# Strassen input sums on one engine, and sums, gate reductions and pairs moved, in a fused decoder-layer kernel

## The chip, the cores and the metric

The kernel runs on one core of a Trainium2 chip. Its inputs and output are in the chip's memory, everything is fp32, and the matrix engine is fed the fp32r type: each operand is split into a high part and a low remainder, and three matmuls (high by high, high by low, low by high) make one product. The metric is the device time of one execution in microseconds (us); lower is better. Three executions of the kernel before took 934.26, 934.66 and 939.55 us.

The engines are called by their profile names: PE is TensorE (matmuls; PEld its weight loads), DVE VectorE, ACT ScalarE, POOL GpSimd, and SP SyncE, whose queue issues nearly all DMAs in order.

## The reference

One decoder layer on 1024 tokens of width 1024, cut to what is computed:

```python
mod = c @ w_ada + b_ada; shift, scale, gate = split(mod, 3)
h = rms_norm(x, g_pre) * (1 + scale) + shift
proj = h @ w_in                 # 5144 columns: queries, keys, values, SiLU gates, merge gates
q_a, kv_c, kv_s, kv_w, g_nsa, z_a, q_b, kv_b, z_b, merge = split(proj, pts)
# mixer A: compressed (an MLP over blocks), selected and window-512 attention, 8 heads, 2 kv heads
o_a = gts[0] * o_cmp + gts[1] * o_slc + gts[2] * o_win
y_a = (merge_heads(o_a) * silu(z_a)) @ w_o_nsa
# mixer B: window-128 attention with sinks, 8 heads, 2 kv heads
o_b = banded_attention(q_b, k_b, v_b, slopes_b, 128, sinks=sinks)
y_b = (merge_heads(o_b) * silu(z_b)) @ w_o_swa
m_a, m_b = split(merge, 2)
y = (sigmoid(m_a) * y_a + sigmoid(m_b) * y_b) @ w_out
out = x + gate * rms_norm(y, g_post)
```

## The kernel before, in words

Features lie on the 128 partitions and tokens along the free dimension, in two halves of 512 tokens. `hh` and `hl` are the high and low parts of the normalised input h, eight blocks of 128 features by two halves. The weight matrix w_in is cut into named blocks of 128 columns: Q and K blocks, `ZA0..3` and `ZB0..3` (SiLU gates), and `MA0..7`, `MB0..7` (merge gates).

The order of the work: normalise x and project values, the first keys and queries (to about 90 us); the Z blocks and the compression MLP (`mlp`, L630, two sides), side by side to about 181 us; then four units of attention, `("B", 0), ("B", 1), ("A", 0), ("A", 1)`, to about 722 us; then the last matrix products with the merge gates and w_out. A scheduler orders the instructions of each engine from priorities (program order, raised or lowered by `high_priority`) and a simulated clock; on the chip each engine and each DMA queue then runs its list in that fixed order, and waits at the first instruction that isn't ready.

**Attention.** A unit runs eight query blocks. `scores` (L790) makes the scores on PE, bias and row minimum on DVE (L862), the exponential on ACT (L874), the row scales (for mixer B with two 128x4 tensor_tensor instructions on DVE, L880 and L882) and the scaling on POOL (L886). `weigh` (L910) transposes on PE (L923), splits on ACT and DVE (L929, L930) and multiplies by V on PE (L931, L934). `finish` (L936) loads the SiLU gate `zt`, adds the two halves of the result into `ot` (ACT L943, DVE L944), multiplies on POOL (L945) and stores; `zt` and `ot` have one buffer each. Between these steps projection products of later Q, K and merge-gate blocks are put in: in the B units whole blocks (`proj_half`, L193, matmuls at L200 to L208, weights split by ACT L174 and POOL L177), in the A units halves of products (`Part`, L969), spaced by a plan in units of PE columns.

**The merge gates by Strassen.** Two of the 16 merge-gate blocks (`PLAIN`, MB0 and MB1) are projected plainly; the other 14 are taken as seven pairs (`PAIRS`). A pair (a, b) is a 2x2 block product with h split into two feature halves and two token halves, done in seven products in place of eight. It needs sums of the four weight quarters (S1 to S4, `pair_sums`, L697: four 128x512 tensor_tensor on POOL, each stored) and sums of the four quarters of h (T1 to T4).

- `early_sums` (L712) makes the weight sums of pairs 0 to 2 ahead of attention, in four of the eight `q` buffers (the first queries hold the other four); `late_sums` (L1139) makes those of pairs 3 to 6 in the B units, two a unit, in `ps` buffers that the scores use too.
- `input_sums(k)` (L719, k = 0 to 3) follows them in the same four `q` buffers: two loads of h, two adds on POOL (L726), four sums on DVE (L727 to L730), then for each T a high part on ACT (L733), the low part on DVE or POOL in turn (L735), and two stores (L736, L737).
- `new_set` (L1035) loads a T, high and low, over parts of `hh` and `hl` that are no longer used, in the last two units. `middle_products` and `last_products` use them; the last products (T3 and T4) of pairs 3 to 6 come behind attention, in the "seam" (L1289 to L1306), where the finished second block of each pair is stored, to be loaded again as a gate.

**The gated products.** Behind the seam eight reductions (L1308 to L1326) make the post-norm gate from w_ada: eight loads of 512 KB and 11 reductions on DVE (L1322). Then `gated` (L1328) runs for m = 0 to 7 on side B and again on side A: it loads a w_o block, makes two products of 12 matmuls (L1336 to L1338), and multiplies each by a merge gate that `merge_gate` (L1273) loads and puts through a sigmoid. Between them the w_out rows are loaded and formed into the sums of another Strassen product.

Of the kernel before, what the change touches and what calls it, by code (L numbers as in the profile page):

```python
# [14 lines left out]
P = 128  # L15
# [50 lines left out]
EARLY = 3  # L66
# [4 lines left out]
def hybrid_kernel(tc, io, out):  # L71
# [84 lines left out]
    t_dram = {n: [[dram.tile([P, HS], F32, name=f"{n}{x}{k}", tag=f"{n}{x}{k}") for x in "hl"] for k in range(KH)]  # L156
# [555 lines left out]
    def early_sums(p):  # L712

        quads = [t.bitcast(F32) for t in spare(4)]
        for t, (name, j) in zip(quads, ((PAIRS[p][0], 0), (PAIRS[p][0], 1), (PAIRS[p][1], 0), (PAIRS[p][1], 1))):
            nc.sync.dma_start(t.rearrange("p (k t) -> p k t", k=KH), quarter_of(name, j))
        pair_sums(p, *quads)
# [218 lines left out]
    def finish(mixer, g, i, pv):  # L936
        zt = at.tile([64, 4, P], F32, name="zt", tag="zt", bufs=1)
# [201 lines left out]
    def late_sums(p):  # L1139

        a, b = (at.tile([P, S], F32, name="ps", tag="ps", bufs=4) for _ in range(2))
        for t, name in zip((a, b), PAIRS[p]):
            nc.sync.dma_start(t.rearrange("p (k t) -> p k t", k=KC), io["w_blk"][W_IDX[name]])
        pair_sums(p, a[:, :HS], a[:, HS:], b[:, :HS], b[:, HS:])
# [547 lines left out]
```

## Time and profile before

| | before |
|---|---|
| time, three executions | 934.26, 934.66, 939.55 us |
| profiled execution: its time, its span | 934.04 us, 931.5 us |
| PE busy | 879.4 us (94%), 4418 matmuls |
| DVE, ACT, POOL busy | 676.9, 530.2, 504.4 us |
| mean granted TensorE clock | 0.974 of full speed |
| DMA | 164.06 MB, mean 176 GB/s |

The span runs from the first instruction to the last; the 2.54 us between span and time lie around it. The profile takes one execution; that one is 0.62 us below the median. "Busy" of PE counts a matmul from its start to a modelled end, and neighbours overlap, so that how fast matmuls follow one another tells more than the busy share. [...]

### The profile page before, as it was taken

The numbers are of one execution on the slowest core, as the hardware profiler recorded it, in microseconds if no ns is written. First come the engines' busy times: TensorE is split into PE (matmuls) and PEld (weight loads), VectorE is DVE, ScalarE is ACT, GpSimd is POOL, SyncE is SP. The second block draws the span as 40 slices with busy tenths as digits, with TensorE's granted clock in tenths as the row PEclk, the third lists the DMA queues.
The fourth block names the chain that finished last, engine by engine and source line by source line (L and its number), as shares of the span: only waits on it lengthen the run. The fifth ranks groups of instructions, "written<-read, shape, count | busy, mean of one in ns | idle before, by whom it ended". The sixth has DMA issues, their size and how long they took to land.

```text
span 931.5 us, 14888 instructions
## 1 busy us (share of the span) xinstructions
PE 879.4 (94%) x4418; PEld 736.0 (79%) x4418; DVE 676.9 (73%) x1651; ACT 530.2 (57%) x1200; POOL 504.4 (54%) x523
## 2 busy tenths in 40 slices
PE   9999989849998989999999999999999969989994
PEld 7889778637887878788888888888887858877884
DVE  5866965884688867766677677777674578788996
ACT  6487423444676687766567686666564237453241
POOL 1001862594876887645346486654553229854541
PEclk9999999959999999999999999999999989999998
DMA  9966684855545543121132754423462899951322
GB/s 352 316 234 216 211 282 170 290 210 151 194 149 168 158 151 108 58 91 69 46 103 67 276 174 127 134 91 114 162 212 91 286 403 342 324 175 35 102 91 113
DMA packets 99058, 164.06 MB, mean 176 GB/s; under 512 B 11553, under 2 KB 29345, under 8 KB 98978
## 3 DMA queue, kind: packets, MB, share of 16 engines
q1 hardware_dynamic: 97824, 161.89, 51.3%
q10 hardware_dynamic: 1154, 1.23, 0.5%
q8 instruction: 35, 0.57, 0.2%
q14 instruction: 45, 0.37, 0.1%
HBM read 115.10 MB, written 44.30 MB: 171 GB/s over the span
## 4 chain that ended last, share of the span: by engine, by line
PE 74%; DVE 12%; DMA 6%; issue 3%; ACT 2%; POOL 2%; SPq 1%; DVEq 0%; POOLq 0%; ACTq 0%
PE b_pt L923 7%; PE b_pj L990 6%; PE b_pj L996 6%; PE b_pj L995 6%; PE b_pv L934 4%; PE b_s L855 4%; PE b_s L852 4%; PE b_pv L931 4%; PE b_pj L200 3%; PE b_pj L207 3%; PE b_pj L208 3%; DMA wa<-in_w_adaT 2%; PE b_s L223 1%; PE b_s L225 1%; PE b_s L224 1%
## 5 line engine op out<-in xcount | busy, mean ns | idle before, releaser
L177 POOL TENSOR_TENSOR wl<-wraw,wh 128x512 fp32r<-128x512 f32 x123 | 167.9, 1370 | 102.3 <-ACT wh L174 72.7
L930 DVE TENSOR_TENSOR pl<-b_pt,ph 128x512 fp32r<-128x512 f32 x162 | 110.4, 686 | 42.0 <-ACT ph L929 41.3
L929 ACT CAST ph<-b_pt 128x512 fp32r<-128x512 f32 x162 | 93.6, 583 | 60.4 <-PE b_pt L923 51.9
L174 ACT CAST wh<-wraw 128x512 fp32r<-128x512 f32 x115 | 70.2, 618 | 52.9 <-PE b_pj L995 24.2
L874 ACT ACTIVATE ps<-ps,mins 128x256 f32<-128x256 f32 (+7 forms) x128 | 81.0, 634 | 32.5 <-DVE mins L862 29.1
L852 PE MATMUL b_s<-kh,q 128*128 128x256 f32 (+6 forms) x272 | 86.8, 327 | 12.0 <-DVE mins L862 11.3
L200 PE MATMUL b_pj<-hh,wh 128*128 128x512 f32 x208 | 84.0, 404 | 9.3 <-ACT wh L174 6.0
L886 POOL TENSOR_SCALAR ps<-ps,rr,gates 128x128 f32<-128x128 f32 (+7 forms) x64 | 52.5, 824 | 65.5 <-DVE rr L878 53.3
L855 PE MATMUL b_s<-kl,q 128*128 128x256 f32 (+6 forms) x272 | 83.5, 316 | 0.0
L208 PE MATMUL b_pj<-hh,wl 128*128 128x512 f32 x208 | 82.7, 399 | 0.6 <-POOL wl L177 0.6
L207 PE MATMUL b_pj<-hl,wh 128*128 128x512 f32 x208 | 82.8, 398 | 0.0
L990 PE MATMUL b_pj<-hh,wh 128*128 128x512 f32 x188 | 77.7, 413 | 0.0
L996 PE MATMUL b_pj<-hh,wl 128*128 128x512 f32 x188 | 74.2, 395 | 0.0
L995 PE MATMUL b_pj<-hl,wh 128*128 128x512 f32 x188 | 74.2, 395 | 0.0
L923 PE MATMUL b_pt<-ident,ps 128*128 128x128 f32 x408 | 69.7, 281 | 1.1 <-POOL ps L886 0.9
L934 PE MATMUL b_pv<-pl,V 128*128 128x512 f32 x162 | 69.3, 428 | 0.4 <-DVE pl L930 0.2
L931 PE MATMUL b_pv<-ph,V 128*128 128x512 f32 x162 | 67.0, 414 | 1.7 <-DVE ot L944 1.5
L852 PEld LDWEIGHTS b_s<-kh,q 128*128 128x128 f32 x272 | 51.7, 190 | 21.2 <-DVE mins L862 13.1
L923 PEld LDWEIGHTS b_pt<-ident,ps 128*128 128x128 f32 x408 | 52.8, 144 | 12.2 <-POOL ps L886 1.7
L886 POOL TENSOR_SCALAR pw<-pw,rr,gates 128x640 f32<-128x640 f32 (+4 forms) x64 | 47.5, 744 | 24.5 <-DVE rr L878 20.1
L855 PEld LDWEIGHTS b_s<-kl,q 128*128 128x128 f32 x272 | 51.8, 191 | 6.6
L200 PEld LDWEIGHTS b_pj<-hh,wh 128*128 128x128 f32 x208 | 40.0, 192 | 18.5 <-ACT wh L174 7.6
(446 smaller groups left out, 2468.7 us busy)
## 6 DMA issues: line engine op xcount, KB each, us to landing
wraw<-in_w_blk SPq DMA_DIRECT2D x83, 256.0 KB, 3.1
wa<-in_w_adaT SPq DMA_DIRECT2D x20, 512.0 KB, 5.2
r<-in_w_out SPq DMA_DIRECT2D x32, 256.0 KB, 5.1
wraw<-sS SPq DMA_DIRECT2D x28, 256.0 KB, 2.9
w1raw<-in_w SPq DMA_DIRECT2D x16, 256.0 KB, 4.0
ps<-in_w_blk SPq DMA_DIRECT2D x8, 512.0 KB, 4.8
sS<-ps SPq DMA_DIRECT2D x16, 256.0 KB, 2.3
od<-ot SPq DMA_DIRECT2D x64, 64.0 KB, 2.1
```

The source lines that it names most:

```text
L177: chain("wl", nc.gpsimd.tensor_tensor(wl, raw, wh.bitcast(F32), ALU.subtract))
L200: ins = nc.tensor.matmul(t, lhsT=wh, rhs=hh[kc][half], start=(kc == 0), stop=False)
L207: nc.tensor.matmul(t, lhsT=wh, rhs=hl[kc][half], start=False, stop=False)
L208: nc.tensor.matmul(t, lhsT=wl, rhs=hh[kc][half], start=False, stop=(kc == KC - 1))
L852: ins = nc.tensor.matmul(sp[:, :n_in], lhsT=q, rhs=rh, start=True, stop=False)
L855: nc.tensor.matmul(sp[:, :n_in], lhsT=q, rhs=rl, start=False, stop=True)
L923: ins = nc.tensor.transpose(t[:, r * P : r * P + P], rows[r][:, off : off + P], ident)
L930: nc.vector.tensor_tensor(pl, t, ph.bitcast(F32), ALU.subtract)
L934: nc.tensor.matmul(pv, lhsT=v, rhs=pl, start=False, stop=(last and n == len(todo) - 1))
L990: ins = nc.tensor.matmul(self.t, lhsT=wh[:, kc, :], rhs=hi, start=(self.first is None and kc == 0), stop=False)
L995: nc.tensor.matmul(self.t, lhsT=wh[:, kc, :], rhs=lo, start=False, stop=False)
L996: ins = nc.tensor.matmul(self.t, lhsT=wl[:, kc, :], rhs=hi, start=False, stop=(kc == KH - 1 and self.stop))
```

## The change

- **Order of the pairs.** `PLAIN` becomes MA6, MA7, and the pairs are (MA0, MA1), (MA2, MA3), (MA4, MA5), then (MB4, MB0) to (MB7, MB3). The seam now finishes MB0 to MB3; it puts them through the sigmoid there and keeps them in SBUF (`early`), where `gated` takes them; they are no longer stored and loaded. T3 and T4 products of a pair follow one another.
- **Weight sums.** None ahead of attention. `late_sums` takes pairs 0 and 1 in the first unit (steps 0 and 4) and pair 2 in the second, at lowered priority. `paced_sums` takes pairs 3 to 6 in the third unit, in `kts` and `kt` buffers, loads and sums at planned points.
- **Input sums.** All six sums of `input_sums` are on POOL, and each T is stored once, not split. `set_load` loads a T into the place of its low part, and `set_form` splits it (ACT copy, POOL subtract) in the last unit, ahead of given parts of the plan.
- **Gate reductions.** The eight w_ada blocks are reduced ahead of attention, behind the input sums, in 16 halves of 128x512 through the three `wraw` buffers, which the weights of the projections use too; c is broadcast into two `kt` buffers.
- **Heads.** `finish` of mixer B takes `zt` and `ot` from the four `pw` buffers, so two of each.

```diff
-PLAIN = ["MB0", "MB1"]
-PAIRS = [("MB2", "MB3"), ("MB4", "MB5"), ("MB6", "MB7")] + [(f"MA{m}", f"MA{m + 4}") for m in range(4)]
+PLAIN = ["MA6", "MA7"]
+PAIRS = [("MA0", "MA1"), ("MA2", "MA3"), ("MA4", "MA5")] + [(f"MB{m + 4}", f"MB{m}") for m in range(4)]
...
+    gate_c, gate_part = [], sm.tile([P, 8], F32, name="gpart")
+    for h in range(2):
+        gate_c.append(kq.tile([P, HS], F32, name="cg", tag="kt", bufs=6))
+        nc.sync.dma_start(gate_c[h], io["c"][h * HS : h * HS + HS].partition_broadcast(P))
+    def gate_sum(k):
+        blk, part = 16 + k, gate_part[:, k : k + 1]
+        for h in range(2):
+            wa = wp.tile([P, HS], F32, name="wraw", tag="wraw", bufs=3)
+            nc.sync.dma_start(wa, io["w_adaT"][blk * P : blk * P + P, h * HS : h * HS + HS])
+            nc.vector.tensor_tensor_reduce(
+                out=wa, in0=wa, in1=gate_c[h], scale=1.0, scalar=part if h else smalls[:, 8 + blk : 9 + blk],
+                op0=ALU.mult, op1=ALU.add, accum_out=mod[:, blk : blk + 1] if h else part)
     def input_sums(k):
...
-            nc.gpsimd.tensor_tensor(t, hh[kk][0].bitcast(F32), hl[kk][0].bitcast(F32), ALU.add)
-        nc.vector.tensor_tensor(b22, b22, b12, ALU.subtract)
-        nc.vector.tensor_tensor(b12, b12, b11, ALU.subtract)
-        nc.vector.tensor_tensor(b11, b22, b11, ALU.add)
-        nc.vector.tensor_tensor(b21, b21, b11, ALU.subtract)
-        for n, (name, t) in enumerate((("T3", tiles[3]), ("T1", tiles[2]), ("T2", tiles[0]), ("T4", tiles[1]))):
-            hi = wp.tile([P, HS], F32R, name="wh", tag="wh", bufs=WBUFS)
-            nc.scalar.copy(hi, t.bitcast(F32))
-            eng = nc.gpsimd if n % 2 else nc.vector
-            eng.tensor_tensor(t, t.bitcast(F32), hi.bitcast(F32), ALU.subtract)
-            nc.sync.dma_start(t_dram[name][k][0], hi.bitcast(F32))
-            nc.sync.dma_start(t_dram[name][k][1], t.bitcast(F32))
-    for p in range(EARLY):
-        early_sums(p)
+            op_(t, hh[kk][0].bitcast(F32), hl[kk][0].bitcast(F32), ALU.add)
+        op_(b22, b22, b12, ALU.subtract)
+        op_(b12, b12, b11, ALU.subtract)
+        op_(b11, b22, b11, ALU.add)
+        op_(b21, b21, b11, ALU.subtract)
+        for name, t in (("T3", b22), ("T1", b12), ("T2", b11), ("T4", b21)):
+            nc.sync.dma_start(t_dram[name][k], t)
     for k in range(KH):
         input_sums(k)
+    for k in range(8):
+        gate_sum(k)
+    nc.vector.tensor_tensor(amod, mod[:, 16:24], g_post, ALU.mult)
...
+        if mixer == "B":
+            zt, ot = (at.tile([64, 512], F32, name=n, tag="pw", bufs=4) for n in ("zb", "ob"))
...
+    def set_form(name, ks):
+        for k in ks:
+            hi, lo = sets[name][k]
+            nc.scalar.copy(hi, lo.bitcast(F32))
+            nc.gpsimd.tensor_tensor(lo, lo.bitcast(F32), hi.bitcast(F32), ALU.subtract)
...
+    def paced_sums(p):
+        quads = {}
+        def get():
+            a11, a12 = (kq.tile([P, HS], F32, name="sa", tag="kts", bufs=8) for _ in range(2))
+            a21, a22 = (kq.tile([P, HS], F32, name="sb", tag="kt", bufs=6) for _ in range(2))
+            quads[0] = a11, a12, a21, a22
+            for n, t in ((2, a21), (3, a22), (0, a11), (1, a12)):
+                nc.sync.dma_start(t.rearrange("p (k t) -> p k t", k=KH), quarter_of(PAIRS[p][n // 2], n % 2))
+        return get, lambda: pair_sums(p, *quads[0])
...
-            for n in range(2):
-                p = EARLY + 2 * u + n
-                if p < NP:
-                    at_step.setdefault(1 + 4 * n, []).append(lambda p=p: late_sums(p))
+            for p in ((0, 1), (2,))[u]:
+                at_step.setdefault(4 * (p % 2), []).append(lambda p=p: late_sums(p))
...
+                for n, p in enumerate(range(FIRST, NP)):
+                    for f, share in zip(paced_sums(p), (0.02, 0.07)):
+                        pieces.append((begun + whole[u] * (share + 0.14 * n), lambda at, f=f: f()))
...
+                for n, (name, ks) in enumerate((("T2", (0, 1)), ("T2", (2, 3)), ("T1", (0, 1)), ("T1", (2, 3)))):
+                    ahead_of(line[2 + n], lambda name=name, ks=ks: set_form(name, ks))
...
+                for k in range(KH):
+                    ahead_of(line[11 + k], lambda k=k: set_form("T3", (k,)))
...
+                ahead_of(e[1][0], lambda: set_form("T4", range(KH)))
...
-            store(half_of(PAIRS[p][1], 1), e)
-            seam.append((p, y))
-        for p, y in seam:
-            t = seam_part(load_half(quarter_of(PAIRS[p][1], 1)), sets["T4"])
+            nc.scalar.activation(e, e, AF.Sigmoid)
+            t = seam_part(load_half(quarter_of(b, 1)), sets["T4"])
             nc.vector.tensor_tensor(y, y, t, ALU.add)
-            store(half_of(PAIRS[p][1], 0), y)
-        cbg = op.tile([P, D], F32, name="cbg", tag="oh3")
...
-                nc.sync.dma_start(wa, io["w_adaT"][blk * P : blk * P + P, n * w : n * w + w])
...
+            nc.scalar.activation(y, y, AF.Sigmoid)
+            early[b, 1], early[b, 0] = e, y
...
+                if (name, half) in early:
+                    sg = early[name, half]
```

## Rows read from the trace of the kernel before

**Rows 1.** The page's head and the busy time of the engines (us, share of the span, instructions).

```profile
span 931.5 us, 14888 instructions
...
PE 879.4 (94%) x4418; PEld 736.0 (79%) x4418; DVE 676.9 (73%) x1651; ACT 530.2 (57%) x1200; POOL 504.4 (54%) x523
```

**Rows 2.** Busy time by stretch. The columns are: the stretch, its length, then busy us (x instructions) of PE, PEld, DVE, ACT and POOL, the granted TensorE clock (1.00 is full speed), the busy share of the 16 DMA engines, and GB/s.

```profile
116.00:140.00 24.00, 20.98 (x89) 16.83 (x88) 14.36 (x17) 6.62 (x10) 14.98 (x12) 0.93 0.85 282
140.00:163.00 23.00, 23.00 (x128) 20.00 (x127) 13.63 (x22) 6.96 (x13) 6.04 (x5) 1.00 0.47 168
...
176.00:210.00 34.00, 17.94 (x70) 13.01 (x69) 30.84 (x58) 17.76 (x49) 29.68 (x32) 0.65 0.70 253
...
280.00:303.00 23.00, 20.53 (x103) 16.92 (x102) 19.18 (x44) 15.01 (x41) 16.00 (x21) 0.93 0.51 163
...
530.00:625.00 95.00, 94.96 (x524) 80.95 (x523) 72.09 (x274) 68.16 (x188) 63.67 (x82) 1.00 0.41 130
...
755.00:770.00 15.00, 7.39 (x26) 5.66 (x25) 12.49 (x24) 7.88 (x14) 6.37 (x4) 0.77 1.05 398
770.00:820.00 50.00, 50.00 (x222) 41.39 (x222) 40.10 (x45) 29.38 (x52) 44.40 (x29) 1.00 0.95 326
```

**Rows 3.** What PE waited for over the whole span: the waiting line, what released it, us in total, times, longest us.

```profile
PE b_s L852 <- DVE mins L862: 11.3, 5, 5.1
PE b_pj L1336 <- ACT wh L174: 7.6, 1, 7.6
PE b_pj L200 <- ACT wh L174: 6.0, 1, 6.0
...
PE b_pv L931 <- DVE ot L944: 1.5, 1, 1.5
```

**Rows 4.** From the timelines of DVE, ACT and POOL near 200 us: start, us from there to the end of the last of the merged instructions, engine, line, what it writes and reads, how many.

```profile
197.23 4.84 DVE L729 TENSOR_TENSOR q<-q 128x512 f32<-128x512 f32 x1
...
203.43 1.66 ACT L174 CAST wh<-wraw 128x512 fp32r<-128x512 f32 x3
...
197.22 1.26 POOL L945 TENSOR_TENSOR ot<-ot,zt 64x512 f32<-64x512 f32 x1
198.46 1.83 POOL L886 TENSOR_SCALAR ps<-ps,rr 128x256 f32<-128x256 f32 x4
200.26 1.26 POOL L735 TENSOR_TENSOR q<-q,wh 128x512 fp32r<-128x512 f32 x1
```

**Rows 5.** The instructions of the input sums, grouped by line, from 80 to 210 us, where all of them lie: count, busy us in total, mean ns of one, idle time of the engine before them and what ended it.

```profile
L735 POOL TENSOR_TENSOR q<-q,wh 128x512 fp32r<-128x512 f32 x8 | 11.1, 1387 | 21.1 <-ACT wh L733 21.1
L726 POOL TENSOR_TENSOR q<-hh,hl 128x512 f32<-128x512 f32 x8 | 10.7, 1338 | 8.2 <-DMA T2l<-q 7.0 <-DMA sS<-q 0.8 <-DMA T4l<-q 0.3
L733 ACT CAST wh<-q 128x512 fp32r<-128x512 f32 x16 | 9.7, 619 | 17.4 <-DVE q L727 6.1 <-issue 3.9 <-DMA T3h<-wh 2.1
...
L735 DVE TENSOR_TENSOR q<-q,wh 128x512 fp32r<-128x512 f32 x8 | 7.9, 1003 | 2.5 <-ACT wh L733 2.5
L729 DVE TENSOR_TENSOR q<-q 128x512 f32<-128x512 f32 x4 | 7.6, 1890 | 0.0
...
L727 DVE TENSOR_TENSOR q<-q 128x512 f32<-128x512 f32 x4 | 4.0, 1011 | 4.3 <-DMA q<-h1d 4.3
L728 DVE TENSOR_TENSOR q<-q 128x512 f32<-128x512 f32 x4 | 3.3, 814 | 0.1
L730 DVE TENSOR_TENSOR q<-q 128x512 f32<-128x512 f32 x4 | 2.7, 681 | 0.0
```

**Rows 6.** From the timelines of DVE and POOL in the second half of the B units; of POOL the first and the last of four instructions in a row (the others are L704 and L177).

```profile
280.76 4.92 DVE L882 TENSOR_TENSOR sums<-sums,rr 128x4 f32<-128x4 f32 x1
...
280.63 1.29 POOL L945 TENSOR_TENSOR ot<-ot,zt 64x512 f32<-64x512 f32 x1
...
284.38 1.27 POOL L706 TENSOR_TENSOR ps<-ps 128x512 f32<-128x512 f32 x1
```

**Rows 7.** Where the stage ahead of attention begins and ends for POOL (its first weight sum, and attention's first scaling), the two last loads into `wraw` ahead of attention on SP's queue, and three kinds of DMA: KB each and median us from issue to landing.

```profile
93.38 3.31 POOL L700 TENSOR_TENSOR q<-q 128x512 f32<-128x512 f32 x1
...
179.72 1.95 POOL L886 TENSOR_SCALAR ps<-ps,rr 128x128 f32<-128x128 f32 x3 [0.41 <-DVE rr L883]
...
139.91 0.33 SPq L164 DMA_DIRECT2D wraw<-in_w_blk  x1
...
143.02 0.33 SPq L164 DMA_DIRECT2D wraw<-in_w_blk  x1
...
wraw<-in_w_blk SPq DMA_DIRECT2D x83, 256.0 KB, 3.1
...
q<-h1d SPq DMA_DIRECT2D x8, 256.0 KB, 3.5
...
T4l<-q SPq DMA_DIRECT2D x4, 256.0 KB, 3.3
```

**Rows 8.** The gate reductions: of the instructions of L1322 the 128x512 ones (ns least/median/most), and SP's queue from 741 us on.

```profile
L1322 DVE CUSTOM_DVE_ANT_0 r<-r,cbg,smalls x3: 746/746/746, 755.8 to 758.7; 128x512 f32<-128x512 f32 x3
...
741.89 3.25 SPq L1320 DMA_DIRECT2D wa<-in_w_adaT  x3
...
750.78 2.90 SPq L1320 DMA_DIRECT2D r<-in_w_adaT  x4
...
756.54 0.33 SPq L164 DMA_DIRECT2D wraw<-in_w_o  x1
```

More of the change, by code (lines that the diff above doesn't have):

```diff
@@ L62 @@
 W_NAMES, W_COLS = w_blocks()
-PLAIN = ["MB0", "MB1"]
-PAIRS = [("MB2", "MB3"), ("MB4", "MB5"), ("MB6", "MB7")] + [(f"MA{m}", f"MA{m + 4}") for m in range(4)]
+PLAIN = ["MA6", "MA7"]
+PAIRS = [("MA0", "MA1"), ("MA2", "MA3"), ("MA4", "MA5")] + [(f"MB{m + 4}", f"MB{m}") for m in range(4)]
 NP = len(PAIRS)
-EARLY = 3
+FIRST = 3
 LOOK = 3
@@ L155, in hybrid_kernel @@
     h_dram = [dram.tile([P, HS], F32, name=f"h1d{k}", tag=f"h1d{k}") for k in range(KC)]
-    t_dram = {n: [[dram.tile([P, HS], F32, name=f"{n}{x}{k}", tag=f"{n}{x}{k}") for x in "hl"] for k in range(KH)]
+    t_dram = {n: [dram.tile([P, HS], F32, name=f"{n}d{k}", tag=f"{n}d{k}") for k in range(KH)]
               for n in ("T1", "T2", "T3", "T4")}
@@ L710, in spare @@
         return [kq.tile([P, HS], F32R, name="q", tag="q", bufs=8) for _ in range(n)]
[L712 to L717, printed above, removed]
+    gate_c, gate_part = [], sm.tile([P, 8], F32, name="gpart")
[10 more added lines that the diff above has]
+                op0=ALU.mult, op1=ALU.add, accum_out=mod[:, blk : blk + 1] if h else part)
     def input_sums(k):
-        tiles = spare(4)
-        b11, b21, b12, b22 = (t.bitcast(F32) for t in tiles)
+        op_ = nc.gpsimd.tensor_tensor
+        b11, b21, b12, b22 = (t.bitcast(F32) for t in spare(4))
         nc.sync.dma_start(b12, h_dram[k])
@@ L936, in finish @@
     def finish(mixer, g, i, pv):
-        zt = at.tile([64, 4, P], F32, name="zt", tag="zt", bufs=1)
+        if mixer == "B":
+            zt, ot = (at.tile([64, 512], F32, name=n, tag="pw", bufs=4) for n in ("zb", "ob"))
+            zt = zt.rearrange("d (r t) -> d r t", r=4)
+        else:
+            zt = at.tile([64, 4, P], F32, name="zt", tag="zt", bufs=1)
+            ot = at.tile([64, 512], F32, name="ot", tag="ot", bufs=1)
         for p in range(2):
@@ L1033, in hybrid_kernel, with set_load @@
     sets = {}
-    def new_set(name, j, half):
-        res = []
+    def set_load(name, j, half):
+        sets[name] = res = []
         for k in range(KH):
@@ L1040, in new_set, with ahead_of, both @@
             pair = [main.tile([P, HS], F32R, name=f"{x}t{kk}", tag=f"{x}{kk}_{half}") for x in ("hh", "hl")]
-            for t, src in zip(pair, t_dram[name][k]):
-                nc.sync.dma_start(t.bitcast(F32), src)
+            nc.sync.dma_start(pair[1].bitcast(F32), t_dram[name][k])
             res.append(pair)
-        sets[name] = res
+    def set_form(name, ks):
[3 more added lines that the diff above has]
+            nc.gpsimd.tensor_tensor(lo, lo.bitcast(F32), hi.bitcast(F32), ALU.subtract)
+    def ahead_of(part, f):
+        was = part.before
+        def both():
+            f()
+            if was:
+                was()
+        part.before = both
     def t_set(name):
@@ L1139, in late_sums @@
     def late_sums(p):
[L1141 to L1144, printed above, removed]
+        with tc.high_priority(offset=-PRIO):
+            a, b = (at.tile([P, S], F32, name="ps", tag="ps", bufs=4) for _ in range(2))
+            for t, name in zip((a, b), PAIRS[p]):
+                nc.sync.dma_start(t.rearrange("p (k t) -> p k t", k=KC), io["w_blk"][W_IDX[name]])
+            pair_sums(p, a[:, :HS], a[:, HS:], b[:, :HS], b[:, HS:])
+    def paced_sums(p):
[7 more added lines that the diff above has]
+        return get, lambda: pair_sums(p, *quads[0])
     late = []
@@ L1209, in hybrid_kernel @@
                                    lambda at, f=f, k=k, ahead=ahead: f.piece(k, at, ahead)))
+            pieces.sort(key=lambda x: x[0])
         prev = None
@@ L1287, in seam_part @@
             return t
-        seam = []
+        early = {}
         for n, p in enumerate(range(NP - 4, NP)):
+            b = PAIRS[p][1]
             if n < 2:
@@ L1338, in gated @@
                     nc.tensor.matmul(ty, lhsT=wo[1][:, k, :], rhs=o_h, start=False, stop=(k == 3))
-                sg = tmp("t2", 4)
-                merge_gate(name, half, sg)
+                if (name, half) in early:
+                    sg = early[name, half]
+                else:
+                    sg = tmp("t2", 4)
+                    merge_gate(name, half, sg)
                 emit(sl, ty, sg)
```

26 lines of the change are left out of this document (4 added, 22 removed).

## The prediction

> **What bounds the kernel now.** I read the page's totals, then busy time by stretch, then what PE waits for, and last the timelines at the places these point to. PE is the bound, and its busy share hides how far from it single stretches are, so I count matmuls. From 140 to 163 us, full clock, PE issues 128 in 23.0 us, 0.18 us each for a mix of shapes; from 770 to 820 us 222 of 512 columns in 50.0 us, 0.225 us each [rows 2]. Against these two paces four stretches stand out:
>
> - 176 to 210 us, the start of attention: 70 matmuls in 34.0 us at a granted clock of 0.65. At 0.18 they need 12.6: **21.4 us lost**.
> - 755 to 770 us, the gated products: 26 in 15.0 us at 0.77. At 0.225 they need 5.9: **9.1 us lost**.
> - 280 to 303 us, in the B units: 2.5 us without a matmul and a clock of 0.93, another 1.6: **4.1 us lost**.
> - 116 to 140 us, Z blocks and MLP: 3.0 us without one and 0.93, another 1.7: **4.7 us lost** [rows 2].
>
> In the A units PE stands still for 0.04 us of 95; nothing is to be had there [rows 2]. In the first stretch PE waits for the row minima on DVE and for ACT's copies of the K weights (11.3 and 6.0 us over the span [rows 3]). Why these are late is in the timelines: DVE's L729, an input sum, takes 4.84 us where L730 takes 0.68, and ends just after a run of POOL instructions, 197.2 to 201.5 us; ACT copies the K weights only at 203.4, behind copies for the input sums that waited for that DVE instruction [rows 4, 5]. So the input sums, standing in DVE's and ACT's lists among attention's first steps, cost most of the 21.4 us. In the second stretch PE waits 7.6 us for a w_o block [rows 3]: its load is issued at 756.5, behind the loads for the gate reductions on SP, with the DMA engines full (share 1.05) [rows 2, 8].
>
> **The change, part by part.** The sum runs against the profiled execution: span 931.5 us [rows 1], and 2.54 around it.
>
> *Input sums.* DVE loses 24 instructions, 7.9 + 7.6 + 4.0 + 3.3 + 2.7 = 25.5 us, ACT 16 copies, 9.7 us, and POOL 8 subtractions, 11.1 us, all ahead of or inside the gap; POOL gains 16 sums at the price of its present adds, 1.34 us, 21.4 us [rows 5]. Stores fall from 32 to 16, and the 12 weight sums of POOL, with 24 DMAs, leave the stage. With one set of four buffers the sums stay a chain: a load 3.5, six sums 8.0, the last store 3.3 us, so 14.8 for each k and 59 for four. From 93.4, where POOL now starts its weight sums, that ends at 153; attention first needs POOL at 179.7 [rows 5, 7]. The 27 us between are room for the Z weights' splits. What then stands in the gap are attention's own steps and a pair of weight sums, as in the other B stretches. The nearest row is 280 to 303 us: 4.1 lost in 23, so 6.1 in 34 us [rows 2]. I take a gain of **15**; the ends are 0 (something else fills the gap) and 21.4.
>
> On this trace the DVE ops that go take 1.06 us each on average, since POOL holds them up, and 0.68 at their fastest, against POOL's 1.34 [rows 5]. [...]
>
> *Gate reductions moved.* 16 x 0.75 = 12 us of DVE [rows 8] come ahead of attention, where 25.5 us leave. Their 16 loads go through three `wraw` buffers ahead of the K weights, whose last two loads ahead of attention now stand at 139.9 and 143.0. A turn is 3.1 + 0.75 us, so 16 / 3 turns take 20.5 us, to 160.4, and K's loads land by 164, well before attention's first scaling at 179.7 [rows 7, 8]; until then PE has Z products. Price **0** under that cover; without it, the second rival.
>
> *Seam and gated products.* Eight loads of 512 KB and c go, eight stores and eight loads of 256 KB too: 8.5 MB, or 21 us at the 398 GB/s of that stretch [rows 2]. The w_o load no longer stands behind them. I take a gain of **8** of 9.1; the 1.1 is for the sigmoid, which now comes earlier on ACT. Ends: 0 and 9.1.
>
> *B units.* Two head buffers take away PE's wait for `ot`, 1.5 us [rows 3]; the second unit has one pair's weight sums instead of two. A lock-out like L882's, 4.92 us behind four POOL instructions [rows 6], becomes rarer, and it is what the 4.1 us are made of. I take a gain of **2**. Ends: 5.6 (both), and a loss of 1.5, since sums at lowered priority may keep two of the four `ps` buffers longer.
>
> *Ahead of attention.* Twelve more sums of POOL, 16 us net, run beside the MLP. From 116 to 140 us PE lost 4.7 us with POOL 15.0 us busy [rows 2]; in proportion that is 5 more. DVE has less to do there, which could give the 4.7 back. I take a loss of **2**, nearer to the upper end, as every POOL sum can hold a DVE one. Ends: a gain of 4.7, a loss of 5.
>
> *A units.* The third gets 16 weight sums, 21.4 us of POOL, the fourth 16 splits, 22.2 us of POOL and 9.7 of ACT [rows 5]. POOL is 67% busy there and PE never waits [rows 2], so most is hidden. The exposed piece is T4's: four splits in a row, 5.5 us, one part of the plan ahead of their use. I take a loss of **2**; ends 0 and 10.9 (that, and four weight sums in a row ahead of a scaling).
>
> Sum: 931.5 - 15 - 8 - 2 + 2 + 2 = 910.5, and 2.5 around it: **913 us**. The profiled execution's time, 934.04, is 0.6 below the median of 934.66, so this is 2.3% below the median. With every term at its lower end it would be 893.
>
> **The rivals.**
>
> *The gap stays, for POOL* (0.10). The 24 sums take longer than 59 us, by the Z splits and by DVE, and still run when attention starts; POOL's list then holds up the scalings. For it: 32 us of work on an engine already 30 of 34 us busy there [rows 2]. Against it: 27 us of room. With the whole gap 928 us, with half of it 920.
>
> *The gap stays, for the weights' buffers* (0.10). If the 16 gate loads come one by one, held by SP's order or by DVE, they take 16 x 3.85 = 62 us, from 139.9 to 201.5, and the K weights are copied about where they are now, at 203.4 [rows 4, 7]. A wait would take the place of the one removed: 928, or 920 with half. Against it: three buffers, and DVE with 9.4 us of idle time from 140 to 163 [rows 2].
>
> *No gain at the seam* (0.08). Heads and w_out rows also load there, and the DMA share is still 0.95 from 770 to 820 us [rows 2]; if the products wait for these, 921.
>
> *Slower: DVE locked out by POOL ahead of attention* (0.06). A gate reduction reads two operands from SBUF, as L729 and L882 do, and these were held 4.2 and up to 4.9 us by runs of POOL instructions [rows 4, 6]. POOL now has runs of six sums. At one sum each 16 reductions wait 16 x 1.34 = 21 us, at 4.8 each 77; halfway 49, of which 9.4 fit into DVE's idle time. The minima of the first scores stand behind them on DVE. That is 913 + 40 = 953, and it decides from 21 us that reach PE.
>
> [...]
>
> **How the numbers follow.** Forecast 0.62, with a range of its own of 903 to 921; better than 899, with the gap nearly closed, 0.04; the rivals 0.34 as given. The range from **899 to 929** leaves out the slower rival, the very good end and some of the bounds at either end. What this kernel's measurement can tell from no change is about 1%, 9.3 us. Below 925.3 lie the forecast, the better end, the seam rival and some six of the twenty parts of the two gap rivals: **0.80**. Within 1% the rest of these: **0.14**. Above: **0.06**.
>
> **What would show it.** Right: from 176 us on no DVE tensor_tensor of the input sums, K's copies on ACT before 180, a clock of 1.00 in place of 0.65; after 735 us no wait of L1336 of several us, and DMA below 0.9. First rival: POOL still in the input sums behind 176. Second: PE's L200 waiting for L174, and `wraw` loads of w_ada on SP behind 176. Third: L1336 waits for DVE's or ACT's heads. Slower: gate reductions far above 0.75 us with the scores' minima behind them. A loss in the A units would show as waits of PE for L177 or L886 where there are none. The prediction is wrong if the gap from 176 closes and the time doesn't follow.

## The result, and the profile after

The changed kernel takes **905.97 us** (median of four runs, 902.27 to 906.57); the kernel before, run beside it on the same chip, 935.82 (934.26 to 939.55). The ratio is **0.967**, with a 95% interval of 0.963 to 0.971. The profiled execution took 906.57 us, with a span of 904.7. Against 913 forecast the gain is 7 us larger, and inside the range. First the head of the page after and its engines [rows 1]:

```profile
span 904.7 us, 14788 instructions
...
PE 872.4 (96%) x4418; PEld 731.0 (81%) x4418; DVE 659.8 (73%) x1637; ACT 530.0 (59%) x1200; POOL 537.4 (59%) x547
```

PE's work is the same 4418 matmuls, DVE has 17 us less and POOL 33 more. Where it tells is in the stretches, the same seven as in [rows 2], columns as there:

```profile
116.00:140.00 24.00, 19.06 (x87) 15.76 (x86) 18.65 (x15) 5.90 (x9) 21.58 (x14) 0.86 0.67 220
140.00:163.00 23.00, 22.15 (x119) 18.59 (x118) 15.89 (x30) 4.28 (x8) 11.99 (x9) 0.97 0.73 234
176.00:210.00 34.00, 33.74 (x170) 27.34 (x170) 19.61 (x61) 18.95 (x53) 23.34 (x27) 1.00 0.64 215
280.00:303.00 23.00, 23.00 (x126) 19.41 (x125) 19.95 (x55) 17.69 (x47) 16.07 (x23) 1.00 0.58 175
530.00:625.00 95.00, 93.19 (x506) 78.79 (x505) 67.87 (x242) 65.19 (x162) 64.88 (x77) 1.00 0.36 113
755.00:770.00 15.00, 15.00 (x68) 12.39 (x67) 14.96 (x15) 8.28 (x14) 15.00 (x9) 1.00 0.96 328
770.00:820.00 50.00, 50.00 (x220) 40.81 (x219) 38.59 (x48) 19.71 (x35) 26.34 (x19) 1.00 0.59 198
```

The gap from 176 us is closed (170 matmuls where there were 70, full clock), and so is the seam (68 for 26). But the stretch from 116 to 140 us got worse: 87 matmuls at a granted clock of 0.86, with POOL busy for 21.6 of 24 us, where [rows 2] has 89 at 0.93 and 15.0. And the last unit of attention, which had nothing to lose, now loses some. The waits of PE say the same: those of [rows 3] are gone or shrunk, and the longest is one ahead of attention, for L563, the product that ends a Z block.

```profile
PE b_pj L200 <- DVE sp L563: 5.2, 2, 4.9
PE b_s L856 <- DVE mins L866: 3.0, 5, 0.9
...
PE b_pv L935 <- ACT ph L933: 1.5, 1, 1.5
```

For a balance over all kernels I count **lost time**: the length of a stretch less what its matmuls need at the pace of their shape at full clock (0.2275 us from start to start for 512 columns, 0.117 for 256, 0.108 for 128, and so on, read off where PE waits for nothing). It holds to about 1 us: values down to -1 stand for nothing lost. By this the gap before is 23.4 us, where the prediction's mean pace gave 21.4. Each row is one profiled execution; time and ratio to the kernel before are of all runs. The rows e1 to e13 are the experiments of the next section. The profiled execution isn't always a middle one: in e3 (912.3 us) and e6 (910.4) it was the longest, in e9 (890.5) the shortest.

| kernel | 93-176 | 176-210 | 210-303 | 303-345 | 489-559 | 722-840 | median us | ratio, 95% interval |
|---|---|---|---|---|---|---|---|---|
| before | 7.0 | 23.4 | 6.7 | 2.4 | 0.2 | 12.3 | 935.8 | 1 |
| after | 14.0 | 1.0 | 0.8 | 6.9 | 6.0 | -0.5 | 906.0 | 0.967 (0.963, 0.971) |
| e1 | 15.4 | 5.5 | 2.9 | 2.7 | 4.8 | -0.7 | 906.6 | 0.971 (0.967, 0.976) |
| e2 | 7.1 | 22.2 | 3.5 | 6.7 | 0.3 | -1.2 | 916.7 | 0.982 (0.978, 0.986) |
| e3 | 10.8 | -0.3 | 1.6 | 7.9 | 4.7 | 7.2 | 909.8 | 0.974 (0.969, 0.979) |
| e4 | 12.7 | 2.3 | 1.8 | 4.0 | 3.5 | -1.0 | 903.0 | 0.967 (0.964, 0.971) |
| e5 | 12.1 | -0.3 | 0.7 | 6.8 | 5.2 | -1.0 | 899.5 | 0.963 (0.961, 0.966) |
| e6 | 13.7 | 2.1 | 0.7 | 7.8 | 5.0 | 1.5 | 906.1 | 0.971 (0.968, 0.974) |
| e7 | 13.4 | 1.3 | 0.6 | 8.1 | 5.7 | -1.0 | 902.9 | 0.966 (0.963, 0.969) |
| e8 | 13.6 | 3.5 | 1.7 | 8.9 | 5.0 | -1.2 | 908.2 | 0.973 (0.970, 0.977) |
| e9 | 1.8 | 0.0 | 1.8 | 5.5 | 4.6 | -0.1 | 893.9 | 0.957 (0.955, 0.959) |
| e10 | 11.8 | 0.6 | 2.6 | 3.6 | 5.2 | -1.0 | 898.9 | 0.962 (0.960, 0.963) |
| e11 | 10.9 | -0.1 | 2.5 | 4.6 | 2.9 | -1.0 | 897.8 | 0.960 (0.959, 0.962) |
| e13 | 2.3 | 4.5 | 11.8 | 8.1 | 2.7 | -1.0 | 905.3 | 0.968 (0.965, 0.970) |

From before to after: 22.4 won in the gap, 12.8 at the seam, 5.9 from 210 to 303 us, 3.5 behind the last matmul (11.66 us from its end to the span's end, now 8.13); lost are 7.0 ahead of attention, 9.2 from 303 to 722 us, and 2.4 in the first 93 us. That makes 26.0 of the 26.8 us between the spans. The first 93 us differ by 2.8 us among these kernels, whose code is nearly the same there (the changed kernel makes its first two input adds at 75 us). Equal code in the last unit loses between 3.5 (e4) and 6.0 us (after) from 489 to 559 us. So a difference of a us or two between two rows can be chance.

### The profile page after: what moved, and what is told of

The parts are those of the page before. It is cut to its first block, busy times and chain, and to the rows that moved or that the text cites. A ratio compares the mean times of both kernels' runs of the same rounds, so it can differ in the third digit from the quotient of the medians.

```text
span 904.7 us, 14788 instructions
## 1 busy us (share of the span) xinstructions
PE 872.4 (96%) x4418; PEld 731.0 (81%) x4418; DVE 659.8 (73%) x1637; ACT 530.0 (59%) x1200; POOL 537.4 (59%) x547
## 4 chain that ended last, share of the span: by engine, by line
PE 74%; DMA 3%; DVE 3%; issue 1%; ACT 1%; POOL 0%; DVEq 0%; POOLq 0%; SPq 0%; ACTq 0%
PE b_pt L927 8%; PE b_pj L998 7%; PE b_pj L1003 6%; PE b_pj L1004 6%; PE b_s L859 4%; PE b_pv L938 4%; PE b_s L856 4%; PE b_pv L935 4%; PE b_pj L200 3%; PE b_pj L207 3%; PE b_pj L208 3%; PE b_s L1363 1%; PE b_s L1361 1%; PE b_s L1362 1%; DMA wraw<-in_w_adaT 1%
## 5 line engine op out<-in xcount | busy, mean ns | idle before, releaser
L177 POOL TENSOR_TENSOR wl<-wraw,wh 128x512 fp32r<-128x512 f32 x123 | 170.0, 1386 | 98.8 <-ACT wh L174 80.9
L934 DVE TENSOR_TENSOR pl<-b_pt,ph 128x512 fp32r<-128x512 f32 x162 | 110.6, 686 | 47.4 <-ACT ph L933 46.5
L933 ACT CAST ph<-b_pt 128x512 fp32r<-128x512 f32 x162 | 93.2, 584 | 59.9 <-PE b_pt L927 50.8
L174 ACT CAST wh<-wraw 128x512 fp32r<-128x512 f32 x115 | 70.6, 617 | 42.6 <-PE b_pj L1003 18.7
L207 PE MATMUL b_pj<-hl,wh 128*128 128x512 f32 x208 | 83.3, 400 | 0.0
L890 POOL TENSOR_SCALAR ps<-ps,rr,gates 128x128 f32<-128x128 f32 (+7 forms) x64 | 52.4, 822 | 50.9 <-DVE rr L882 42.2
L927 PE MATMUL b_pt<-ident,ps 128*128 128x128 f32 x408 | 67.3, 274 | 0.4 <-DVE pl L934 0.4
L890 POOL TENSOR_SCALAR pw<-pw,rr,gates 128x640 f32<-128x640 f32 (+4 forms) x64 | 47.4, 742 | 22.4 <-DVE rr L882 19.6
L878 ACT ACTIVATE pw<-pw,mins 128x640 f32<-128x640 f32 (+4 forms) x64 | 44.5, 695 | 18.2 <-DVE mins L866 18.0
```

The lines of the kernel that those rows point to most:

```text
L177: chain("wl", nc.gpsimd.tensor_tensor(wl, raw, wh.bitcast(F32), ALU.subtract))
L207: nc.tensor.matmul(t, lhsT=wh, rhs=hl[kc][half], start=False, stop=False)
L878: nc.scalar.activation(rows[r][:, :off], rows[r][:, :off], AF.Exp, scale=-1.0, bias=last_min[:, r : r + 1], accum_out=sums[:, r : r + 1])
L927: ins = nc.tensor.transpose(t[:, r * P : r * P + P], rows[r][:, off : off + P], ident)
L934: nc.vector.tensor_tensor(pl, t, ph.bitcast(F32), ALU.subtract)
```

## The experiments

All are edits of the changed kernel; the theories are in the expectations, as written before each run.

**e1, the weight sums back ahead of attention.**

```diff
+    for p in range(3):
+        early_sums(p)
     for k in range(KH):
         input_sums(k)
...
-            for p in ((0, 1), (2,))[u]:
+            for p in ((3, 4), (5, 6))[u]:
...
-                for n, p in enumerate(range(FIRST, NP)):
-                    for f, share in zip(paced_sums(p), (0.02, 0.07)):
```

> The changed kernel, with three pairs of weight sums again ahead of the input sums and four in the two B units, none in the third unit; the input sums stay in their new form, on GpSimd alone. Theory 1 (time: the start of attention is free because the input sums now end before it): GpSimd gets to the input sums only at about 136 us as before and is in them until about 195, so of the 22 us won in 176 to 210 us at least 8 are lost again, PE waits there for the row minima or for K's copies, and the time is 914 to 925 us. Theory 2 (form: what held attention up was the share of DVE and ACT in the input sums): the stretch loses 4 us at most, and the time is 903 to 911 us.

906.6 us. The input sums end only at 201.4 us, inside attention, and the stretch loses 5.5 us, not 23:

```profile
200.09 1.31 POOL L745 TENSOR_TENSOR q<-q 128x512 f32<-128x512 f32 x1
```

```profile
176.00:210.00 34.00, 29.89 (x149) 23.73 (x149) 22.26 (x51) 14.30 (x40) 29.69 (x29) 1.00 0.76 245
```

So with the new form at most 4.5 of the 22.4 us come from the earlier start; the rest is the form of the sums. The third unit, without weight sums, loses 2.7 us from 303 to 345 in place of 6.9.

**e2, the input sums in their old form, with the early start.** `input_sums`, its stores and the loads of the sets as before; `set_form` empty.

> The changed kernel, with the input sums in their old form (subtractions on DVE, high parts copied on ACT, low parts on DVE and GpSimd, 32 stores, sets loaded already split), but starting where the changed kernel starts them, with no weight sums ahead. Theory 1 (time): four turns of 17 us from 95 us end at about 163, before attention, the stretch 176 to 210 us loses 4 us at most, and the time is 902 to 912 us, the lower end if the fourth unit's stalls for the splits go (3 to 5 us). Theory 2 (form): DVE and ACT are late again at the start of attention, 8 us or more are lost there, 914 us or more.

916.7 us: the gap is back (22.2 us), with a granted clock of 0.66.

```profile
176.00:210.00 34.00, 21.42 (x75) 13.97 (x74) 27.13 (x66) 19.81 (x56) 27.98 (x27) 0.66 0.78 283
```

It isn't DVE alone: the first turn's sums are done by 98.5 us, but their first high copy comes at 149.3 on ACT, behind the steps of the Z blocks and the MLP; the second turn's subtractions begin at 168.6, and POOL's last split ends at 210. Begun some 45 us earlier than before, the old sums end no earlier (205 us before).

```profile
97.78 0.69 DVE L738 TENSOR_TENSOR q<-q 128x512 f32<-128x512 f32 x1
...
149.32 0.62 ACT L741 CAST wh<-q 128x512 fp32r<-128x512 f32 x1 [1.51 <-PE b_pj L207]
152.04 0.62 ACT L741 CAST wh<-q 128x512 fp32r<-128x512 f32 x1 [2.10 <-PE b_pj L207]
...
157.57 0.62 ACT L741 CAST wh<-q 128x512 fp32r<-128x512 f32 x1 [3.67 <-DVE q L743]
161.17 0.62 ACT L741 CAST wh<-q 128x512 fp32r<-128x512 f32 x1 [2.98 <-DMA T1h<-wh]
...
168.61 1.20 DVE L735 TENSOR_TENSOR q<-q 128x512 f32<-128x512 f32 x1 [2.48 <-DMA sp_ZA<-sp]
```

ACT isn't full: from 98.5 to 149.3 us it is busy for 19.2 of 50.8. What the four copies of the first turn wait for last is a `wh` buffer: L207 multiplies by the `wh` of a Z block, L743 and the store read the `wh` of an earlier copy. The high copies share the six `wh` buffers with the Z weights and stand behind these in the program, so the first splits wait until Z products, and then each other's steps, let go of these. No run gave them buffers of their own, so ACT's order and the buffers are not told apart.

The size of the gap is that of before, but not the waits: from 176 to 212 us PE waits 5.7 us for POOL's scalings and 3.5 for row minima, and not for K's copies; the kernel before waits there 8.9 us for the minima and 6.0 for the copies.

```profile
PE b_pt L932 <- POOL ps L895: 5.7, 3, 2.6
PE b_s L861 <- DVE mins L871: 3.5, 3, 2.6
```

The other result: with no splits in the last unit, 489 to 559 us loses 0.3 in place of 6.0.

**e5, four of six sums on DVE, not split.**

```diff
-        op_(b22, b22, b12, ALU.subtract)
+        nc.vector.tensor_tensor(b22, b22, b12, ALU.subtract)
```

and so for the other three subtractions and sums.

> The changed kernel with four of the six input sums of each turn on DVE again, but not split: no copies on ACT, no low parts, 16 stores. Theory 1 (the splits in ACT's queue stretched the old sums from 95 us to 204, into attention; DVE's share by itself is harmless): the sums end before 165 us, 176 to 210 us loses 3 us at most, and GpSimd's 21 us less ahead of attention take 2 to 6 us from the 11 lost from 116 to 176 us: 899 to 905 us. Theory 2 (DVE's share is what holds attention up): 8 us or more are lost again from 176 to 210 us, 912 us or more.

899.5 us, and nothing lost from 176 to 210 us. The last sum ends at 140.3:

```profile
139.60 0.69 DVE L738 TENSOR_TENSOR q<-q 128x512 f32<-128x512 f32 x1
...
176.00:210.00 34.00, 34.00 (x174) 28.49 (x173) 22.07 (x63) 21.70 (x61) 24.17 (x30) 1.00 0.63 209
```

DVE's sums were harmless by themselves; what carried the old ones into attention was splitting them when made. The edit takes out the copies on ACT, the low parts and 16 stores together; that it went by way of the `wh` buffers and ACT's list is read from e2's trace. The stage ahead of attention still loses 12.1 us, in another way: PE waits 4.3 us for DVE's L643, a step of the MLP, which now shares DVE's list with the sums.

**e9, the sums' arithmetic left out.** Loads and stores stay; T2 and T4 get T3's and T1's tiles.

> The changed kernel without the arithmetic of the input sums: the 24 sums on GpSimd are left out, the loads and the 16 stores stay (T2 and T4 get the same tiles as T3 and T1). If the loss from 116 to 140 us (6.7) is DVE and GpSimd holding each other up, or SP's stores waiting for a sum: it falls to 2 us or less, and PE's wait of 4.9 us for a Z block's product is gone; 898 to 903 us. If it is the transfers of this stage (those of the sums beside W1 and the Z blocks): 4 us or more stay, 903 to 907 us.

893.9 us, less than either theory had. Ahead of attention 1.8 us are lost in place of 14.0:

```profile
93.00:116.00 23.00, 23.00 (x125) 19.91 (x125) 18.95 (x21) 14.53 (x20) 11.20 (x8) 1.00 0.97 331
116.00:140.00 24.00, 23.50 (x121) 19.69 (x121) 14.91 (x29) 8.47 (x13) 4.08 (x3) 1.00 0.60 213
```

From 116 to 140 us 121 matmuls for 87; and the transfers, which now wait for no sum, fill the DMA engines ahead of that (share 0.97) and cost PE nothing. So the price of the sums here is 12 us, and it is in the arithmetic. The timelines of the changed kernel show how, on DVE, POOL, SP and PE:

```profile
127.20 2.29 DVE L635 TENSOR_TENSOR fl<-flat,fh 128x2048 fp32r<-128x2048 f32 x1 [1.04 <-PE b_pj L208]
129.41 1.52 DVE L171 CAST wh<-wraw 128x512 fp32r<-128x512 f32 x1
130.84 1.78 DVE L643 TENSOR_TENSOR w<-w1raw,w 128x512 fp32r<-128x512 f32 x1
132.54 1.35 DVE L651 TENSOR_SCALAR he<-he 126x256 f32<-126x256 f32 x1
133.81 1.48 DVE L171 CAST wh<-wraw 128x512 fp32r<-128x512 f32 x1
135.21 1.74 DVE L652 RECIPROCAL he<-he 126x256 f32<-126x256 f32 x1
136.87 0.62 DVE L563 SCALAR_TENSOR_TENSOR sp<-sp,b_pj 128x512 f32<-128x512 f32 x1
...
127.28 4.79 POOL L734 TENSOR_TENSOR q<-hh,hl 128x512 f32<-128x512 f32 x2 [1.68 <-DMA T2d<-q]
...
133.76 0.33 SPq L740 DMA_DIRECT2D T3d<-q  x1
...
137.55 0.79 PE L200 MATMUL b_pj<-hh,wh 128*128 128x512 f32 x1 [4.94 <-DVE sp L563]
```

DVE runs here without a pause, and four of its instructions are stretched beside POOL's, three beside sums and the second L171 beside L177 (133.7 to 135.0 us): the two L171 take 1.5 us (0.41 at their fastest), L643 1.78 (0.68), L651 1.35 (0.29). PE waits 4.9 us for the L563 at their end. POOL's two adds take 4.8 us in place of 2.7 (twice the 1.34 of [rows 5]), and SP's list stops from 128.7 to 133.8 at a store that waits for a sum. What of the 12 us is DVE's stretched steps and what is SP's stop was not told apart. How far DVE is stretched, the changed kernel's L643 tells, from 93 to 163 us:

```profile
L643 DVE TENSOR_TENSOR w<-w1raw,w 128x512 fp32r<-128x512 f32 x13 | 17.0, 1337 | 0.9 <-ACT w L642 0.9
```

and the same in e9:

```profile
L643 DVE TENSOR_TENSOR w<-w1raw,w 128x512 fp32r<-128x512 f32 x13 | 9.7, 765 | 1.6 <-ACT w L642 1.6
```

**e8, the high copies of the weights ahead of attention on ACT.**

```diff
-            ins = nc.vector.tensor_copy(wh, raw)
-            after(ins, last["dve"])
+            ins = nc.scalar.copy(wh, raw)
+            after(ins, last["act"])
```

> The changed kernel with the high copies of the weights ahead of attention on ACT in place of DVE. If the loss from 116 to 140 us is DVE held up by GpSimd's sums (its steps from 127 to 137 us took 10.0 us without a pause): DVE's list is two or three copies of 1.5 us shorter there, PE's wait of 4.9 us for the gating product of a Z block falls to 2 us or less, and the time is 901 to 905 us. If it is the GpSimd sums that hold up SP (its stores wait in order for the sums, the Z blocks' loads and stores behind them), the wait stays at 4 to 5 us, and the time is 904 to 908 us.

908.2 us, where the first theory had 905 at most. PE's wait for L563 falls to 1.8 us as the first theory has it, but 13.6 us are lost all the same: 5.5 from 93 to 116 us, and a wait of 2.6 us for the copies themselves, on ACT. The wait moved, so this run doesn't decide between the two.

**e13, the sums moved into the B units** (with e5, e4 and e11 below).

```diff
-    for k in range(KH):
-        input_sums(k)
...
+            for n in range(2):
+                at_step.setdefault(((2, 6), (3, 5))[u][n], []).append(lambda k=2 * u + n: late_inputs(k))
```

> Run e11's kernel with the input sums (four on DVE, two on GpSimd a turn, not split) taken out of the stage ahead of attention and set into the B units, two turns in each, at lowered priority and in the four buffers of the windowed rows, which the B units with one head buffer don't use. Run e9 showed that without the sums the stretch 93 to 176 us loses 1.8 us, in e11 it loses 10.9. If the B units have room for them: 93 to 176 us falls to 4 us or less (the gate reductions stay there), 176 to 303 us loses 5 us at most, and the time is 888 to 893 us. If the price goes with the sums (they hold up DVE and GpSimd in the B units as before the change): 176 to 303 us loses 9 us or more, and the time is 896 to 905 us.

905.3 us. The price goes with the sums: 2.3 us lost ahead of attention, but 16.3 from 176 to 303 us, where e11 loses 2.4.

```profile
116.00:140.00 24.00, 24.00 (x124) 20.44 (x123) 15.39 (x28) 7.39 (x11) 5.39 (x4) 1.00 0.45 151
...
210.00:303.00 93.00, 88.14 (x442) 72.94 (x441) 64.80 (x183) 60.79 (x169) 69.52 (x86) 0.96 0.50 160
```

**e3, the gate reductions back in the tail**, `gate_sum` left out, the loop of before put in front of `gated`.

> The changed kernel, with the gate reductions and their 4.5 MB of loads back between the seam and the gated products; the early gates stay in the chip's memory. Theory 1 (the seam's 9 us went to these loads, which stood ahead of w_o on SP): 5 to 9 us are lost again from 745 to 770 us, waits of PE for the w_o splits come back, the DMA share there is above 0.95; the stretch 116 to 176 us gains 0 to 4 of the 7 us that it lost; together 907 to 915 us. Theory 2 (the seam gained by the gates no longer stored and read back): under 2 us lost at the seam, 902 to 908 us.

909.8 us. From 722 to 840 us 7.2 are lost, most from 770 on; PE waits for w_o's copies there (3.9 us, the line that [rows 3] has with 7.6):

```profile
PE b_pj L1363 <- ACT wh L174: 3.9, 2, 3.2
```

Ahead of attention 3.2 us come back (1.9 against e4, which has the same code there). Net, the move of the reductions is worth 4.5 us by these two traces; the two ratios' intervals overlap, so the time doesn't show it.

**e6, the early gates stored and read back**, with the reductions left ahead of attention: the seam of before, without its reductions.

> The changed kernel with the early gates' sums stored to DRAM and read back at the gated products, as before (4 MB), and the gate reductions left ahead of attention. Run e3 showed that the reductions' loads by themselves cost some 6 us from 770 to 840 us. Theory 1 (the other 7 of the 13 us won at the seam came from these stores and loads): 4 to 7 us are lost again from 745 to 840 us, 909 to 913 us. Theory 2 (only the two together are too much for the transfers): under 2 us are lost, 904 to 908 us.

906.1 us, as after; the seam loses 2.0 us more than after in the trace, which is of the longest execution. Of the 12.8 us won there, the reductions' move gives 7.7 and the kept gates 2.0, each by itself; the other 3.1 come with neither alone. The 2.0 are not shown in the time.

**e4, one head buffer.**

```diff
-        if mixer == "B":
-            zt, ot = (at.tile([64, 512], F32, name=n, tag="pw", bufs=4) for n in ("zb", "ob"))
...
+        zt = at.tile([64, 4, P], F32, name="zt", tag="zt", bufs=1)
+        ot = at.tile([64, 512], F32, name="ot", tag="ot", bufs=1)
```

> The changed kernel with one head buffer and one gate buffer in the B units, as before, no longer in the buffers of the windowed rows. If the second buffer is worth its forecast: PE's waits for the head buffer come back, 1 to 2 us lost from 210 to 303 us, 907 to 909 us. If it only moves a wait to the start of the third unit, where the first windowed rows wait for the last head's store (1.95 us on DVE at 318 us): that wait goes, PE loses 2 us less from 303 to 345, and the time is 904 to 907 us.

903.0 us, the same ratio. The trace has both: 210 to 303 us loses 1.0 more, 303 to 345 us 2.9 less. The second is well clear of chance: from 303 to 345 us the kernels with paced sums and one head buffer (e4, e10, e11) lose 3.6 to 4.6 us, those with paced sums and two 5.5 to 8.9; e13, which has one but puts input sums in the windowed rows' places, loses 8.1. The two buffers lie in the places of the first windowed rows, and these wait for the last head's store, while POOL stands at the first planned weight sum:

```profile
317.83 0.29 DVE L866 CUSTOM_DVE_ANT_0 pw<-b_s,DC 128x128 f32<-128x128 f32 x1 [1.95 <-DMA od<-ob]
...
317.12 1.27 POOL L700 TENSOR_TENSOR sb<-sb 128x512 f32<-128x512 f32 x1 [3.26 <-DMA sb<-in_w_blk]
```

These lines are of the changed kernel. e1, with two buffers and no weight sums there, loses 2.7; it takes both to lose 7 us.

**e7, the splits of T1 and T3 later in the plan.**

```diff
-                    ahead_of(line[11 + k], lambda k=k: set_form("T3", (k,)))
+                    ahead_of(line[14 + 2 * k], lambda k=k: set_form("T3", (k,)))
```

and T1's from parts 4 and 5 to 5 and 6.

> The changed kernel with the splits of T1 one part of the plan later and those of T3 three to six parts later, so that their loads have landed when ACT comes to them. If the fourth unit's loss is ACT standing at a copy that waits for a load: ACT's waits for T1 and T3 (3.6 and 1.0 us) go, PE's loss of 6 us from 489 to 559 us falls to 1 to 3, and the time is 901 to 904 us. If it is the copies and splits themselves (22 us of GpSimd, 10 us of ACT), the loss moves along with them, and the time stays at 904 to 908 us.

902.9 us, with 5.7 us lost from 489 to 559: it tells nothing of the stall, since the edit didn't move the copies. They ran at 498.4 and 501.1 us, at 501.3 in the changed kernel. As I read it, the scheduler takes the copies as soon as it reckons their loads landed; on the chip they land later, and the next `ph` stands behind the waiting copy:

```profile
501.29 0.62 ACT L1056 CAST hht<-hlt 128x512 fp32r<-128x512 f32 x1 [3.62 <-DMA hlt<-T1d]
501.82 0.58 ACT L933 CAST ph<-b_pt 128x512 fp32r<-128x512 f32 x1
...
502.45 0.51 PE L935 MATMUL b_pv<-ph,V 128*128 128x512 f32 x1 [1.55 <-ACT ph L933]
```

These lines are of the changed kernel, ACT and PE.

**e10, e5 and e4 together.**

> The changed kernel with four of six input sums on DVE, unsplit (run e5), and one head buffer (run e4). If both gains are of their own place, ahead of attention (e5: 6 us) and at the start of the third unit (e4: 3 us): 895 to 898 us, with 303 to 345 us losing 4 us in place of 6.8. If e4's gain was noise of the loads: 898 to 901 us.

898.9 us: 303 to 345 us loses 3.6, as expected, but 210 to 303 us 1.9 more than e5. The time isn't told apart from e5's.

**e11, e10 with the splits held to the plan.**

```diff
-            nc.scalar.copy(hi, lo.bitcast(F32))
+            after(nc.scalar.copy(hi, lo.bitcast(F32)), hold[0])
```

with `hold[0]` set ahead of `self.before()` in `Part.piece`.

> Run e10's kernel with the ACT copies of the fourth unit's splits tied to their place in the plan (each ordered behind the matmul of attention that stands 3 us ahead of its part). In e7 they were moved in the plan and ran at 498 to 503 us all the same, so their place there didn't set when ACT came to them. If ACT's standing at copies that wait for loads makes the loss from 489 to 559 us (4 to 6 us here, none in e2, which has no splits): no wait of ACT for T1 or T3 over 0.5 us, the loss falls to 2 us or less, 2 to 4 us less than e10. If the splits cost PE by their bulk: the same time as e10 within 1.5 us.

897.8 us. T1's and T2's copies now run from 512 us on; of the 16, only two of T4's still wait for a load (1.2 us together). 489 to 559 us loses 2.9, e10 5.2. The other kernel with held splits, e13, loses 2.7 there, the ten that have splits not held 3.5 to 6.0. The time is 1.1 us less, with overlapping intervals: the stall is shown in the trace, its price of 2 us is not shown in the time. What is left there, some 2.6 us over e2, goes with the splits themselves; how was not tried. e11 beats both kernels: 0.960 (0.959 to 0.962) against 0.967 (0.963 to 0.971) for the change as it was.

## Why the prediction was right, and where it was off

**The gap (gain 15; measured 22.4 by shapes, nearly all of it).** The reading was right: the sums' steps among attention's first ones made it, and e2 brings its size back whole, if by other waits. e1 shows that the earlier start matters little. The step that was off is the price of what then stands there: "a pair of weight sums, as in the other B stretches" at 6.1 us. 1.0 was lost; late sums at lowered priority cost attention nothing here. Which part of the old form was guilty was not settled by the rows: I named DVE's list and ACT's list. e5 clears DVE's sums, and what is left is the splitting. The `wh` buffers, for which the first splits wait in e2 and, by the trace, in the kernel before too, I had not looked at:

```profile
152.67 0.62 ACT L733 CAST wh<-q 128x512 fp32r<-128x512 f32 x1 [1.74 <-PE b_pj L207]
```

**POOL's chain (to 153 us).** Its first two adds ran at 75 us, its first subtraction at 94.8, and its last sum ended at 154.1:

```profile
152.83 1.29 POOL L738 TENSOR_TENSOR q<-q 128x512 f32<-128x512 f32 x1
```

**Gate reductions moved (price 0).** They ran from 141 to 174 us, not to 160, waiting for loads, and ACT copied attention's first weights from 174.8 on. PE had Z products until then, so the cover held for the start of attention; but e3 puts their price ahead of it at 2 to 3 us. The second rival's wait didn't come.

**Seam (gain 8; measured 12.8).** Right in kind, w_o's wait is gone. The size is off because 4.1 us lost from 820 to 840 us stood in no term. "DMA below 0.9" failed (0.96 from 755 to 770 us), and it did no harm: PE waited for nothing there.

**B units (gain 2; 5.9) and A units (loss 2; 9.2).** Both terms were mis-sized, and belong together. The price came due at the turn between them, which neither term looked at: head buffers in the windowed rows' places and a POOL sum waiting at the head of its list, 4.5 us (e4, e1). The splits of the last unit cost nearly 6 us by the traces of after and e2 (equal code loses as little as 3.5), some 2 of them ACT standing at a load in order (e11). I had looked for it in POOL's share (T4's four splits ahead of their use) and in waits for L177 or L890; it came through ACT, with no such wait.

**Ahead of attention (loss 2, ends a gain of 4.7 and a loss of 5; measured a loss of 7.0).** The step that failed is "DVE has less to do there, which could give the 4.7 back". DVE had fewer instructions and more busy time, 18.7 us of 24 for 14.4, as POOL's sums stretch those that run beside them: L643 takes 1.54 us on average from 116 to 140 us, 1.20 before, and from 93 to 163 us 1.34, 1.00 before, 0.77 in e9. (Two more L643 also fall into the first of these stretches.) The slower rival had this mechanism, on the gate reductions; it struck the MLP's splits and Z's copies, for 7 us more than before, not 40. e9 puts the whole price of the sums there at 12.2 us, and e13 shows that a price goes with them to where they are put. How much of the 12.2 comes by the stretched steps, and how much by SP's stops at stores, stays open.

By the traces the sums are cheaper on DVE: where neither was stretched, L738 took 0.69 us on DVE (e5) and 1.29 on POOL (the changed kernel), and e5, which puts 16 of the 24 on DVE, has the gap closed just as well (-0.3 us lost from 176 to 210, against 1.0).

**Behind the last matmul (no term; gain 3.5).** It stays in e3, so it isn't the reductions. That part takes 7.9 to 10.0 us in the other kernels; the cause was not tried.

## What to carry to other kernels

Work that is off the critical path is dear where its steps stand in another engine's in-order list ahead of something late: splitting at the place of use instead of when made kept ACT's list and the weights' `wh` buffers out of this chain, and that, more than the choice of engine or the earlier start, closed the gap (23.4 us before, 22.2 in e2 with the old form, 5.5 in e1 with the late start, -0.3 in e5 with the sums on DVE). Price a POOL stream also by how far it stretches DVE's instructions beside it (from 93 to 163 us L643 took 1.34 us on average with the sums on POOL, 0.77 in e9 without them), not by POOL's own room alone, and look at the turn from one stage to the next when buffers are shared (303 to 345 us lost 6.9 us, 2.4 before). A low-priority step with a load ahead of it needs a tie to the plan, or, as I read it, the scheduler puts it where the load should have landed (ACT stood 3.62 us at a load of T1 in the changed kernel; with the splits tied 489 to 559 us lost 2.9 in e11, 5.2 in e10 without).

## What the runs showed of the hardware

Which DVE instructions POOL stretches could be read here, and I hadn't expected copies among them. In the changed kernel L171, a copy with one operand in SBUF, took 0.41 to 1.52 us, and L651, which adds a constant, 0.29 to 1.35, beside L643 with two, 0.68 to 1.78. In e9, without the sums, L651 took 0.29 both times. Two lines that read PSUM weren't: L934 took 0.67 to 0.69 in all of 162 (0.69 at 330.3 us, beside POOL's L177), L563 0.62 to 0.69 in 16 (0.69 at 121.0 us, beside POOL's L736). Nor was L652, a reciprocal of one operand in SBUF: 1.74 us beside POOL's L177, 1.75 in e9.
